# Gate tiles squared ahead inside the group loop, and weight parts in three pairs, in a two-layer FNet/attention kernel

## The chip, the cores and the metric

One core of a Trainium2 chip runs the whole program. The metric is the device time of one execution in microseconds; lower is better. Engines are called by the names that the profile uses: PE (TensorE: matmuls), ACT (ScalarE), DVE (VectorE), POOL (GpSimd) and SP (SyncE, which here only issues transfers). PEclk is the share of full clock granted to PE.

## The reference, cut to what matters

Two layers on 256 tokens of width 2048, with a second stream of 256 context tokens. The change lies in layer 0, the Fourier layer, in its gate and in its output projection, and in the rows of `silu(c) @ ada_w` that are needed later.

```python
def _fourier_branch(h, w_in, w_mix):            # w_in: 2048 x 8192
    u, z = jnp.split(h @ w_in, 2, axis=-1)      # z is the gate: 4096 columns
    ug = u.reshape(b, n, 16, 256)
    f = jnp.fft.fft2(ug, axes=(1, 3), norm='ortho').real
    f = jnp.einsum('bngc,gcd->bngd', f, w_mix).reshape(b, n, D_BRANCH)
    return f * jax.nn.silu(z)

for i in range(DEPTH):
    shift, scale, gate = jnp.split((jax.nn.silu(c) @ ada_w[i] + ada_b[i])[:, None, :], 3, axis=-1)
    h = _rmsnorm(x, norm_g[i]) * (1 + scale) + shift
    ...
    x = x + gate * (y @ w_out[i])
```

All weights are float32. The kernel keeps the precision by splitting each operand in a high and a low part and adding three products, `mm3`: high·high, high·low, low·high.

## The kernel before

**The loop over 16 groups.** After an opening stage, the loop over g computes one group of 256 branch columns per turn, some 14.4 us each (118 to 332 us of the span). Per turn SP loads two 1 MB tiles of the Fourier half of the input weights (`raw<-in_wu`), DVE folds them (`wm`, and in place `wp`, L134), ACT casts the high parts (`wmh`, `wph`, L66), DVE subtracts for the low parts (L67), and PE multiplies. Two more operands come by way of ACT and DVE: the mixing weights of the turn (`m` is loaded by ACT's queue, DVE adds and subtracts to `mt`, ACT casts it to a high part `mh<-mt`, L66, and PE transforms it with the constants `ch`, `cl`; the results are `pqh`, `sp`), and PE's sums (`mh<-ps` and `aph<-ps`, L66; `ml` and `apl` are DVE's low parts, L67). PE mixes both, and ACT copies `gsb` (L694) and a column of `ft` (L700) out. In turns 8 to 11 a 1 MB gate tile (`wz0`) is also loaded into the shared ring of three `raw` buffers, and ACT squares it (L161, 128x2048) with a sum per row, in place. The sum gives the power-of-two-like scale under which the 16-bit split of a gate tile is made (POOL adds over the partitions, L165 `tot`; DVE makes the scale `up` and its inverse `dn`, L170 and L171; ACT multiplies `dn` with a second factor, L173).

**Shared gate tiles.** Four `wz0` tiles (kg 0 to 3) give four gate blocks of 128 columns each (332 to 382 us). The 16 operands hs(k) come from transfers that POOL issues (`act<-in_xT`, L762): DVE scales (L768), ACT casts to 16 bits (L769), DVE subtracts (L770). Each tile is split in two halves by ACT (L179) and DVE (L180). The 1 MB loads alternate between the ring `raw` and a second ring `rawz` of three buffers.

**Units.** Then come 28 tiles `wz` (382 to 672 us) and 32 tiles `wo0` (672 to 1004 us), each with 48 matmuls of 128x512. The tile after next is loaded, squared by ACT into the buffer that will hold its own high part (L161 `w<-raw`), summed by POOL, and split by ACT and DVE (L179, L180). High and low parts take turns in the few `ws` buffers, so the square of a tile waits for the matmuls of an earlier unit. Between the splits DVE computes rows of `ada_w` (L730, a custom multiply and sum, 128x1024 each; `ada_step` issues up to two steps per unit), from tiles that come through the same two rings, and multiplies the outputs (L780, L870).

**What sets the order.** Each engine runs its instructions in one list, and a waiting instruction holds all behind it. The list is made by a scheduler from the program's order, with `issue_after(x)` as a bound: what stands inside is not listed ahead of x. SP's and POOL's transfers are issued in order too.

Of the kernel before, what the change touches and what calls it, by code (L numbers as in the profile page):

```python
# [10 lines left out]
F32 = mybir.dt.float32  # L11
# [21 lines left out]
def tile_dit(ctx: ExitStack, tc: tile.TileContext, a: dict, out: bass.AP):  # L33
# [134 lines left out]
    def scale(tot, down=None, tag="", bufs=6):  # L168
        u, d = small("up" + tag, bufs=bufs), small("dn" + tag, bufs=bufs)
        V.tensor_scalar(u.bitcast(I32), tot.bitcast(I32), -0.5, float(204 << 23), op0=ALU.mult, op1=ALU.add)  # L170
        V.reciprocal(d, u)  # L171
        if down is not None:
            S.activation(d, d, AF.Copy, scale=down)  # L173
        return u, d
# [397 lines left out]
    w4 = adap.tile([P, 4], F32, name="w4")  # L572
    hsc = adap.tile([P, 2, KT, 2], F32, name="hsc")
    hq = [small("hq") for _ in range(3)]
    squares(hsc[:, 0], gs0, hq[0], 64.0)
    squares(hsc[:, 1], sh0, hq[1], 1.5)
    V.tensor_tensor(hq[2], hq[0], hq[1], op=ALU.add)
    hup, hdn = scale(total(hq[2]), None, "h", 1)
    V.tensor_scalar(hsc[:, 0], gs0, hup, None, op0=ALU.mult)
    V.tensor_scalar(hsc[:, 1], sh0, hup, None, op0=ALU.mult)  # L580
# [11 lines left out]
    for g in range(G):  # L592
# [36 lines left out]
        if g == 13:  # L629
            w1 = small("w1", bufs=1)  # L630
            V.tensor_reduce(w1, w4, axis=AX.X, op=ALU.add)
# [8 lines left out]
        if g > 3:  # L640
            with after_evac(g - 1), tc.issue_after(m_end[0]), tc.issue_after(m_end[1]):
                w[1]["p"] = split_part("p", v)
        oa = {} if g > 2 else ou[g]
# [36 lines left out]
        evacs.append((last_cast[0], last_sub[0]))  # L680

# [34 lines left out]
    def ada_jobs():  # L716
        for pieces in ((0,), (1, 2, 3)):
            for kh in range(2):
                cb = adap.tile([P, 2, 1024], F32, tag="cb", name="cb")
                with tc.issue_after(hs_end[2]):  # L720
                    nc.gpsimd.dma_start(cb, a["crow"][:, kh].broadcast_to([P, 2, 1024]))
                with tc.issue_after(hs_end[1]):
                    S.activation(cb, cb, AF.Silu)  # L723
                for i in pieces:
                    for fg in range(8):
                        w = ada_raw(a["adw"][i, kh, fg])
                        for f in range(2):
                            wf = w[:, f * 1024 : f * 1024 + 1024]
                            for s in range(2 if i < 3 else 1):
                                V.tensor_tensor_reduce(junk, wf, cb[:, s], 1.0, 0.0, ALU.mult, ALU.add, acc[:, i, kh, fg * 2 + f, s : s + 1])  # L730
# [10 lines left out]
    junk = adat.tile([P, 1056], BF16, name="junk")[:, 0:1024]  # L741
    acc = adat.tile([P, 4, 2, KT, 2], F32, name="acc")
    YA = 8
    with tc.tile_pool(name="yp", reuse_waits="tile", bufs=33 - YA) as ypool, tc.tile_pool(name="zp", reuse_waits="tile", bufs=3) as zp:
        ys = [act() if b < YA else ypool.tile([P, 512], F32, tag="y", name="y") for b in range(NB)]
        hs = []
        hs_end = [None] * 3
        turn = [0]

        def raw6(src, view=lambda t, s: ((t, s),)):  # L750
            turn[0] += 1
            pool, nm = (rawp, "raw") if turn[0] % 2 else (zp, "rawz")
            t = pool.tile([P, D], F32, tag=nm, name=nm)
            for d, s in view(t, src):
                last_dma[0] = nc.sync.dma_start(d, s).ins
            return t

        ada_raw = raw6
# [14 lines left out]
        yq = adap.tile([P, NB], F32, name="yq")  # L773
# [26 lines left out]
        ready = {}  # L800

        def fetch(n):
            if n >= len(jobs):
                return
            nm, at_, i = jobs[n]
            if nm == "wz":
                t = raw6(a["wz"][at_])
            else:
                v = a["wo0"][at_[0] // 8, i * 8 : i * 8 + 8].rearrange("g p (j b f) -> p g j b f", j=2, b=8)[:, :, :, at_[0] % 8]
                t = raw6(v, lambda t, s: [(t.rearrange("p (g j f) -> p g j f", g=8, j=2)[:, :, j], s[:, :, j]) for j in range(2)])  # L810
            h, q = half16(), small("wq")
            squares(h, t, q)
            ready[n] = t, h, *scale(total(q), hdn if nm == "wz" else ydn[i])

        def weights(n):
            t, wh, up_, dn = ready.pop(n)
            wl = half16()
            split16(wh, wl, t, up_)
            fetch(n + 2)
            return wh, wl, dn  # L820

        o4 = [psum() for _ in range(4)]
        for kg in range(4):
            wr = raw6(a["wz0"][kg])
            wh, wl = half16(), half16()
            for i in range(2):
                make_hs(kg * 4 + i * 2)
                q = slice(i * 1024, (i + 1) * 1024)
                with tc.issue_after(hs_end[0]) if kg else nullcontext(), tc.issue_after(hs_end[1]) if kg else nullcontext():
                    split16(wh[:, q], wl[:, q], wr[:, q], u4)  # L830
                make_hs(kg * 4 + i * 2 + 1)
            for j in range(4):
                k = kg * 4 + j
                for b in range(4):
                    q = slice(j * 512 + b * P, j * 512 + (b + 1) * P)
                    mm3(o4[b], wh[:, q], wl[:, q], hs[k][0], hs[k][1], k == 0, k == KT - 1)
        for b in range(4):
            with tc.issue_after(last_dma[0]):
                nc.sync.dma_start(ys[b], fd[b])
        for b in range(4):  # L840
            z_out(b, o4[b], d4)
        fetch(0)
        fetch(1)
        for b in range(4, NB):
            wh, wl, dn = weights(b - 4)
            with tc.issue_after(last_dma[0]):
                nc.sync.dma_start(ys[b], fd[b])
# [9 lines left out]
            with tc.issue_after(hs_end[0]) if b < 8 else nullcontext():  # L857
                ada_step(1)
# [4 lines left out]
        def evac0(b, i, o, dn):  # L863
            t = xin[b]
            gd = adap.tile([P, 2], F32, tag="gd", name="gd", bufs=4)
            V.tensor_scalar(gd, gt0[:, b, :], dn, None, op0=ALU.mult)
# [22 lines left out]
        for n, (b, i) in enumerate(outs):  # L889
            if n == 0:  # L890
                y_scale(1)
            wh, wl, dn = weights(n + NB - 4)
# [10 lines left out]
            ada_step(0 if n > 29 else 2 if n > 19 else 1)  # L903
# [14 lines left out]

    def x1_turn(tb, c):
# [4 lines left out]
        S.copy(t, o)  # L924
        nc.sync.dma_start(x1d[tb, :, c * 512 : (c + 1) * 512], t)

    row_sums(3)
# [8 lines left out]
    with tc.issue_after(st_end[0]):  # L936
# [6 lines left out]
        for c, tb in ((0, 0), (0, 1), (1, 0), (1, 1), (2, 0)):  # L943
            x1_turn(tb, c)
# [593 lines left out]
```

## Time and profile before

| | us |
|---|---|
| median of three runs | 1788.28 |
| lowest and highest run | 1785.28, 1790.5 |
| the profiled execution, own time | 1785.5 |
| its span, first to last instruction | 1783.7 |
| PE busy in the span | 1731.1 (97%) |
| DVE, ACT, POOL busy | 1398.2, 1039.3, 256.6 |

| stage | from, to (us of the span) |
|---|---|
| opening | 0, 118 |
| group loop | 118, 332 |
| shared gate tiles | 332, 382 |
| 28 wz units | 382, 672 |
| 32 wo0 units | 672, 1004 |
| norm, and layer 1 | 1004, 1784 |

The profiled execution is 2.8 us below the median and close to the lowest run. A row of the table of windows gives, for a stretch of the span, the busy time and the number of instructions of each engine, the granted clock and the share of the DMA engines. In a timeline row the bracket is the idle time of that engine ahead of the instruction, and what ended it. In the list of waits a row gives the waiting instruction, whom it waited for, the sum, the count, and the longest.

### The profile page before, as it was taken

What the parts mean: (1) busy time and instruction counts of PE and PEld (TensorE: products, weight loads), DVE (VectorE), ACT (ScalarE), POOL (GpSimd) and SP (SyncE); (2) the same over time, 40 slices, a digit from 0 to 9 for tenths busy, and PEclk for the clock granted to TensorE, in tenths of its full rate; (3) what the DMA queues carried; (4) which work ended last, traced back from release to release, by engine and by line L of the source; (5) the groups of instructions that cost most, each with busy time, mean ns of one, the idle gap of its engine ahead of it and who ended that gap; (6) DMA issues with size and microseconds to landing.
All of it is one profiled execution on the core that took longest, in us unless ns stands there. A gap on an engine that the chain in (4) does not pass through costs nothing. (4 is left out here: it accounts for less than half of the span.)

```text
span 1783.7 us, 25965 instructions
## 1 busy us (share of the span) xinstructions
PE 1731.1 (97%) x9449; PEld 1204.6 (68%) x9449; DVE 1398.2 (78%) x2415; ACT 1039.3 (58%) x1708; POOL 256.6 (14%) x277
## 2 busy tenths in 40 slices
PE   6999999999999999999999999999999999999997
PEld 4679999644444444444444588788888888887886
DVE  5779778789889997953587463989999999997455
ACT  5544544485565656444334343777888888887343
POOL 0002111211000001100101000322212212234001
PEclk9999999999999999999999999999999999999999
DMA  9998898857777798654468323578898988888554
GB/s 393 417 340 230 234 279 237 288 214 283 275 261 264 259 327 256 204 164 130 131 226 275 112 97 104 174 179 219 213 208 211 216 208 208 210 216 262 197 179 142
DMA packets 267777, 403.06 MB, mean 226 GB/s; under 512 B 152641, under 2 KB 218577, under 8 KB 236161
## 3 DMA queue, kind: packets, MB, share of 16 engines
q1 hardware_dynamic: 243584, 363.39, 64.9%
q0 software_dynamic: 19920, 31.06, 6.9%
q10 hardware_dynamic: 4144, 6.95, 1.2%
q8 instruction: 74, 1.21, 0.3%
q14 instruction: 55, 0.44, 0.1%
HBM read 356.26 MB, written 12.59 MB: 207 GB/s over the span
## 5 line engine op out<-in xcount | busy, mean ns | idle before, releaser
L67 DVE TENSOR_TENSOR wl<-raw,wh 128x1024 fp32r<-128x1024 f32 x205 | 272.3, 1334 | 112.0 <-ACT wh L66 109.3
L66 ACT CAST wh<-raw 128x1024 fp32r<-128x1024 f32 x205 | 214.2, 1046 | 136.9 <-PE ps L80 123.6
L730 DVE CUSTOM_DVE_ANT_0 junk<-rawz,cb 128x1024 bf16<-128x1024 f32 x200 | 244.0, 1220 | 8.5 <-ACT cb L723 5.6
L80 PE MATMUL ps<-act,w 128*128 128x512 f16 x640 | 243.5, 381 | 0.5 <-DVE act L770 0.5
L79 PE MATMUL ps<-act,w 128*128 128x512 f16 x640 | 239.4, 381 | 4.0 <-ACT w L179 2.2
L81 PE MATMUL ps<-act,w 128*128 128x512 f16 x640 | 239.6, 379 | 0.2 <-DVE w L180 0.2
L1203 PE MATMUL ps<-h,wh 128*128 128x512 f32 x512 | 187.1, 403 | 0.0
L81 PEld LDWEIGHTS <-w 128*128 128x128 f16 x1024 | 100.2, 98 | 127.9 <-DVE w L180 6.8
L79 PEld LDWEIGHTS <-w 128*128 128x128 f16 x1024 | 100.4, 98 | 125.2 <-ACT w L179 3.3
L80 PEld LDWEIGHTS <-w 128*128 128x128 f16 x1024 | 100.4, 98 | 120.6 <-issue 0.8
L180 DVE SCALAR_TENSOR_TENSOR w<-raw,up,w 128x2048 f16<-128x2048 f32 (+1 forms) x58 | 131.8, 2274 | 51.5 <-PE ps L80 45.1
L161 ACT ACTIVATE w<-raw 128x2048 f16<-128x2048 f32 x54 | 102.8, 1904 | 94.2 <-PE ps L81 50.0
L81 PE MATMUL ps<-y,w 128*128 128x512 f16 x384 | 145.2, 379 | 4.0 <-DVE w L180 4.0
L80 PE MATMUL ps<-y,w 128*128 128x512 f16 x384 | 145.4, 379 | 0.0
L79 PE MATMUL ps<-y,w 128*128 128x512 f16 x384 | 144.9, 379 | 0.0
L1205 PE MATMUL ps<-h,wl 128*128 128x256 f32 x512 | 138.4, 281 | 0.0
L179 ACT ACTIVATE w<-raw,up 128x2048 f16<-128x2048 f32 (+1 forms) x58 | 112.1, 1935 | 23.3 <-DVE up L170 22.2
L80 PE MATMUL ps<-wl,h 128*128 128x512 f32 x320 | 125.1, 391 | 0.3 <-DVE wl L67 0.3
L81 PE MATMUL ps<-wh,h 128*128 128x512 f32 x320 | 123.8, 390 | 0.0
L79 PE MATMUL ps<-wh,h 128*128 128x512 f32 x320 | 122.4, 397 | 0.0
L165 POOL PARTITION_ALL_REDUCE tot<-wq x60 | 42.6, 713 | 541.5 <-ACT w L161 456.8
L1257 DVE SCALAR_TENSOR_TENSOR f<-p,sm,f 128x512 f16<-128x512 f32 x128 | 103.1, 824 | 12.0 <-ACT f L1256 11.8
(380 smaller groups left out, 4051.7 us busy)
## 6 DMA issues: line engine op xcount, KB each, us to landing
raw<-in_wz SPq DMA_DIRECT2D x65, 1024.0 KB, 5.3
rawz<-in_adw SPq DMA_DIRECT2D x56, 1024.0 KB, 5.1
raw<-in_awp SPq DMA_DIRECT2D x32, 1024.0 KB, 12.8
raw<-in_wq SPq DMA_DIRECT2D x32, 1024.0 KB, 5.2
raw<-in_wu SPq DMA_DIRECT2D x32, 1016.0 KB, 7.3
raw<-in_wo SPq DMA_DIRECT2D x54, 512.0 KB, 5.7
raw<-in_wo1b SPq DMA_DIRECT2D x16, 1024.0 KB, 4.9
act<-in_xT POOLq DMA_DIRECT2D x32, 256.0 KB, 6.3
```

The source lines that it names most:

```text
L66: last_cast[0] = S.copy(h, src).ins
L67: last_sub[0] = eng.tensor_tensor(l, src, h.bitcast(F32), op=ALU.subtract).ins
L79: PE.matmul(o, wh, xh, start=start, stop=False)
L80: PE.matmul(o, wh, xl, start=False, stop=False)
L81: return PE.matmul(o, wl, xh, start=False, stop=stop).ins
L161: sq_ins[0] = S.activation(dump, src, AF.Square, scale=scale, accum_out=col).ins
L179: last_cast[0] = S.activation(h, src, AF.Copy, scale=up).ins
L180: last_sub[0] = V.scalar_tensor_tensor(l, src, up, h, op0=ALU.mult, op1=ALU.subtract).ins
L730: V.tensor_tensor_reduce(junk, wf, cb[:, s], 1.0, 0.0, ALU.mult, ALU.add, acc[:, i, kh, fg * 2 + f, s : s + 1])
L1203: PE.matmul(o[0], wh[:, q], hx1[k], start=k == 0, stop=k == KT - 1)
L1205: PE.matmul(o[0][:, 0:N], wl[:, q], hx1[k][:, 0:N], start=False, stop=False)
L1257: V.scalar_tensor_tensor(f[:, 512:1024], pt[tb], sm[:, tb : tb + 1], f[:, 0:512], op0=ALU.mult, op1=ALU.subtract)
```

## The change

**Squares ahead.** Six gate tiles are squared inside the loop: the four `wz0` tiles and the first two `wz` tiles. Each is read in an even turn from 4 to 14 into a buffer of its own (`cb`), not into the ring, and squared in two halves in the odd turn after it. The tiles are loaded once more when they are split, so two tiles are read twice that were read once before. The sums of gs0 and sh0 and their scale move from ahead of the loop into turns 6 and 7.

**Rings.** Weight tiles now all come through `raw`, `ada_w` tiles all through `rawz`. The gate's blocks 0 to 10 (0 to 7 before) are loaded into `act` buffers, and these are taken one by one, not all ahead of the shared tiles.

**Three pairs.** High and low part are taken as a pair at the split, and squares are dumped into a buffer of their own (`sqd`). With the six `ws` buffers three pairs stand at once. Per unit ACT splits tile n and then squares tile n+1; tile n+3 is loaded. The multiply of `dn` (L173) moves from ACT to DVE.

**Other.** Two `ada_step`s are issued in units b = 7, 10, 13; in the 32 `wo0` units the second steps stand in other places, none in the first four. The gate row times the two `dn` of y is made once (`gty`). One transpose of `x1` moves ahead of the last row sums.

```diff
@@ scale
         if down is not None:
-            S.activation(d, d, AF.Copy, scale=down)
+            V.tensor_scalar(d, d, down, None, op0=ALU.mult)
@@ ahead of the loop
-    squares(hsc[:, 0], gs0, hq[0], 64.0)
-    squares(hsc[:, 1], sh0, hq[1], 1.5)
...
+    def read_ahead(j):
+        src = a["wz0"][j] if j < 4 else a["wz"][j - 4]
+        ahead[0] = adap.tile([P, D], F32, tag="cb", name="cb")
+        nc.sync.dma_start(ahead[0], src)
+
+    def square_ahead(j):
+        for i in range(2):
+            t = ahead[0][:, i * 1024 : (i + 1) * 1024]
+            squares(t, t, w6[:, j * 2 + i : j * 2 + i + 1])
@@ in the loop
-        if g == 13:
-            ...
-            u4, d4 = scale(total(w1), hdn, "4", 1)
-        if 8 <= g < 12:
-            t = raw(a["wz0"][g - 8])
-            squares(t, t, w4[:, g - 8 : g - 7])
...
         evacs.append((last_cast[0], last_sub[0]))
+        if g in (4, 6, 8, 10, 12, 14):
+            with tc.issue_after(last_dma[0]):
+                read_ahead(g // 2 - 2)
+        elif g > 4:
+            with after_evac(g):
+                square_ahead(g // 2 - 2)
...
@@ units
-            pool, nm = (rawp, "raw") if turn[0] % 2 else (zp, "rawz")
+        def ada_raw(src):
+            t = zp.tile([P, D], F32, tag="rawz", name="rawz")
...
-            h, q = half16(), small("wq")
-            squares(h, t, q)
-            ready[n] = t, h, *scale(total(q), hdn if nm == "wz" else ydn[i])
+        def measure(n):
+            if n < 2:
+                ready[n] = first[n]
+            elif n < len(jobs):
+                q = small("wq")
+                with tc.issue_after(last_cast[0]):
+                    squares(sqd, loaded[n], q)
+                    tot = total(q)
+                with tc.issue_after(last_sub[0]):
+                    ready[n] = scale(tot, hdn if jobs[n][0] == "wz" else None)
 
         def weights(n):
-            t, wh, up_, dn = ready.pop(n)
-            wl = half16()
-            split16(wh, wl, t, up_)
-            fetch(n + 2)
+            up_, dn = ready.pop(n)
+            wh, wl = half16(), half16()
+            split16(wh, wl, loaded.pop(n), up_)
+            measure(n + 1)
+            fetch(n + 3)
...
-                with tc.issue_after(hs_end[0]) if kg else nullcontext(), tc.issue_after(hs_end[1]) if kg else nullcontext():
+                with tc.issue_after(hs_end[0] if kg else wp_end[1]), tc.issue_after(hs_end[1] if kg else wp_end[0]):
                     split16(wh[:, q], wl[:, q], wr[:, q], u4)
...
-                ada_step(1)
+                ada_step(2 if b in (7, 10, 13) else 1)
...
-            ada_step(0 if n > 29 else 2 if n > 19 else 1)
+            ada_step(0 if n < 4 or n > 28 else 2 if 4 < n < 9 or n > 24 else 1)
```

The first place is ACT in the loop. Before, in the third of the four turns with a gate tile, its square stands ahead of the casts `wmh` and `mh<-mt` (L66; in the turn ahead of it, it stands between `wmh` and a copy of `ft`, with `mh<-mt` behind that):

```order
L66 CAST mh_1459<-ps 127x2x127
L694 COPY gsb<-ps 128x256 x2
L700 COPY ft<-ps 128x2 x2
L161 ACTIVATE raw,w_1403<-raw 128x2048
L66 CAST wmh<-wm 128x1016
L66 CAST mh<-mt 128x512
L436 DMA m<-in_wm 128x512
L66 CAST aph<-ps 127x260
```

Now, in turn 5 and in each odd turn after it, two half squares stand behind the cast of `aph`, ahead of that of `pqh` (`pqh` and `sp` are parts of the mixing weights):

```order
L66 CAST wmh<-wm 128x1016
L66 CAST mh<-mt 128x512
L436 DMA m<-in_wm 128x512
L728 COPY ft<-ps 128x2 x2
L66 CAST wph<-raw 128x1016
L66 CAST aph<-ps 127x260
L161 ACTIVATE cb,w_1403<-cb 128x1024 x2
L66 CAST pqh<-ps 128x512
```

The square has moved from a place ahead of `wmh` and `mh<-mt` to one behind them and behind `aph`. On SP, each read of a gate tile still stands between two `raw<-in_wu` loads, but it goes into a buffer that no such load uses.

The second place is ACT where the loop ends and the shared tiles begin. L769 (now L804) makes the 16-bit halves of hs(k), two per k. Before, the first half of k = 1, the third in the list, is the last one ahead of the `mh<-ps` of turn 15:

```order
L769 ACTIVATE act<-act,hsc 128x256 x2
L694 COPY gsb<-ps 128x256 x2
L700 COPY ft<-ps 128x2
L701 DMA fd_1447<-ft 128x512
L700 COPY ft<-ps 128x2
L701 DMA fd_1448<-ft 128x512
L769 ACTIVATE act<-act,hsc 128x256
L66 CAST mh_1459<-ps 127x2x127
```

Now the split of the first shared tile comes first, and five halves stand ahead of that `mh`:

```order
L179 ACTIVATE w_4153<-raw,up_3882 128x1024 x2
L804 ACTIVATE act<-act,hsc 128x256 x2
L722 COPY gsb<-ps 128x256 x2
L804 ACTIVATE act<-act,hsc 128x256 x2
L728 COPY ft<-ps 128x2
L729 DMA fd_1433<-ft 128x512
L728 COPY ft<-ps 128x2
L729 DMA fd_1434<-ft 128x512
L804 ACTIVATE act<-act,hsc 128x256
L66 CAST mh_1445<-ps 127x2x127
L804 ACTIVATE act<-act,hsc 128x256
L66 CAST aph<-ps 127x260
```

So `mh` has moved behind the whole of k = 1 and half of k = 2.

The third place is ACT at the end of the shared tiles. Before, the squares of the first two `wz` tiles and their splits stand among the last halves of hs:

```order
L179 ACTIVATE w_4428<-rawz,up_3534 128x1024
L161 ACTIVATE w_4540,wq<-raw 128x2048
L161 ACTIVATE w_4552,wq<-rawz 128x2048
L769 ACTIVATE act<-act,hsc 128x256 x2
L179 ACTIVATE w_4540<-raw,up 128x2048
L173 ACTIVATE dn<-dn,dnh 128x1
L179 ACTIVATE w_4552<-rawz,up 128x2048
L769 ACTIVATE act<-act,hsc 128x256 x2
```

Now no square stands there, and the order of the units follows, split, then the square of the next tile (L815 and the `act,yq` rows make the gate's output and its square sum):

```order
L804 ACTIVATE act<-act,hsc 128x256 x4
L179 ACTIVATE w_4429<-raw,up_3882 128x1024
L804 ACTIVATE act<-act,hsc 128x256 x2
L179 ACTIVATE w_4549<-raw,up_4133 128x2048
L751 ACTIVATE cb<-cb 128x2048
L815 ACTIVATE act<-ps,dn_3883 128x512
L179 ACTIVATE w_4619<-raw,up_4142 128x2048
L815 ACTIVATE act<-ps,dn_3883 128x512 x3
L161 ACTIVATE sqd,wq<-raw 128x2048
L161 ACTIVATE act,yq<-act 128x512 x4
L179 ACTIVATE w_4695<-raw,up 128x2048
L161 ACTIVATE sqd,wq<-raw 128x2048
```

The two whole squares have left the stretch in which PE waits for halves of hs, and the splits of the first two units have moved behind nearly all of these halves.

More of the change, by code (lines that the diff above doesn't have):

```diff
@@ L569, in tile_dit, with scale_ahead @@
         fill_pe(len(fill))
-    w4 = adap.tile([P, 4], F32, name="w4")
+    w6 = adap.tile([P, 12], F32, name="w6")
     hsc = adap.tile([P, 2, KT, 2], F32, name="hsc")
-    hq = [small("hq") for _ in range(3)]
-    squares(hsc[:, 0], gs0, hq[0], 64.0)
-    squares(hsc[:, 1], sh0, hq[1], 1.5)
[L577 to L580, printed above, removed]
+    ahead, early = [None], {}
+    def read_ahead(j):
[6 more added lines that the diff above has]
+            squares(t, t, w6[:, j * 2 + i : j * 2 + i + 1])
+    def scale_ahead(j, n, tag):
+        w1 = small("w1", bufs=3)
+        V.tensor_reduce(w1, w6[:, j * 2 : (j + n) * 2], axis=AX.X, op=ALU.add)
+        return total(w1), tag
     fd = [dram.tile([P, 512], F32, name=f"fd{b}") for b in range(NB)]
@@ L771, in make_hs @@
             hs.append((hl[:, 0:512], hl[:, 512:1024]))
-        yq = adap.tile([P, NB], F32, name="yq")
+        yq = adat.tile([P, NB], F32, name="yq")
+        gty = [adat.tile([P, KT, 2], F32, name=f"gty{i}") for i in range(2)]
         yup, ydn, yy = [None] * 2, [None] * 2, []
@@ L891, in tile_dit @@
                 y_scale(1)
+                for d, y in zip(gty, ydn):
+                    V.tensor_scalar(d, gt0, y, None, op0=ALU.mult)
             wh, wl, dn = weights(n + NB - 4)
@@ L923, in x1_turn @@
         t = act()
-        S.copy(t, o)
+        turn_end[0] = S.copy(t, o).ins
         nc.sync.dma_start(x1d[tb, :, c * 512 : (c + 1) * 512], t)
-    row_sums(3)
+    with tc.issue_after(e), tc.issue_after(sq_end[0]):
+        x1_turn(0, 0)
+    with tc.issue_after(turn_end[0]):
+        row_sums(3)
     ssum = [const.tile([P, 4], F32, name=f"ssum{i}") for i in range(2)]
```

87 lines of the change are left out of this document (54 added, 33 removed).

## The prediction

> **What bounds the kernel now.** I read the page first, then PE's waits, then the stretches around them.
>
> ```profile
> span 1783.7 us, 25965 instructions
> PE 1731.1 (97%) x9449; PEld 1204.6 (68%) x9449; DVE 1398.2 (78%) x2415; ACT 1039.3 (58%) x1708; POOL 256.6 (14%) x277
> ```
>
> PE is busy 97% of the span, and the change leaves its matmuls as they are. So only two things can go: moments in which PE waits, and the slow clock behind some of them. PE's list of waits from 215 to 1020 us, the part that the change touches from its first gate tile to its last unit, has these rows:
>
> ```profile
> PE ps L79 <- ACT mh L66: 7.0, 3, 3.7
> PE ps L81 <- DVE w L180: 4.2, 4, 1.5
> PE ps L79 <- ACT w L179: 2.2, 1, 2.2
> PE ps L79 <- ACT act L769: 1.6, 1, 1.6
> PE ps L79 <- ACT ft L700: 1.2, 1, 1.2
> PE ps L885 <- ACT act L872: 1.0, 1, 1.0
> PE ps L80 <- DVE act L770: 0.5, 1, 0.5
> PE ps L80 <- DVE ml L67: 0.4, 1, 0.4
> ```
>
> They sum to 18.1 us. The clock adds to it; the table of windows shows it in PEclk, the third number from the end:
>
> ```profile
> 241.00:245.00 4.00, 4.00 (x23) 4.00 (x22) 2.01 (x3) 0.00 (x0) 0.00 (x0) 0.57 1.17 298
> 272.00:276.00 4.00, 3.44 (x29) 3.45 (x30) 3.98 (x7) 2.34 (x5) 1.46 (x3) 1.00 0.81 132
> 344.00:348.00 4.00, 1.83 (x7) 0.54 (x5) 1.16 (x1) 1.15 (x1) 0.00 (x0) 0.85 0.53 200
> 348.00:352.00 4.00, 4.00 (x15) 1.57 (x14) 3.47 (x9) 2.50 (x5) 0.00 (x0) 0.72 0.80 285
> ```
>
> Behind the wait of 3.7 us the clock is 0.57 for 4 us: 4 × 0.43 = 1.7 us lost. Behind that of 2.2 us at 346.86 it is 0.85 and then 0.72: 0.6 + 1.1 = 1.7 us. Behind that of 2.1 us at 272.56 it is 1.00. So about 21.5 us can go at most, 1.2% of the time.
>
> The Trainium skill, "TensorE: Matmul & The Clock Gate", Part 1, says that the clock halves after an idle window of about 3.4 us. The first and third place agree; at 346.86 a wait of 2.2 us was enough here, so the rule would value that wait at 1.7 us less. The rows decide.
>
> **The loop.** Here is ACT around the wait of 3.73 us, and PE's row:
>
> ```profile
> 236.25 1.91 ACT L161 ACTIVATE raw<-raw 128x2048 f32<-128x2048 f32 x1 [0.68 <-DMA raw<-in_wz]
> 238.15 1.02 ACT L66 CAST wmh<-wm 128x1016 fp32r<-128x1016 f32 x1
> 239.08 0.61 ACT L66 CAST mh<-mt 128x512 fp32r<-128x512 f32 x1
> ...
> 239.75 0.39 PE L79 MATMUL ps<-mh,ch 128*128 128x256 f32 x1 [3.73 <-ACT mh L66]
> ```
>
> ACT waited for the gate tile's transfer, squared for 1.9 us, and only then cast the two operands that PE wanted. The gate tiles cost in a second way: they hold one of three `raw` buffers. The wait at 272.56 comes from this: no square stands right ahead of it on ACT, but the `wu` tile that DVE folds there had to wait for the buffer of the last gate tile, and DVE for the `wu` tile:
>
> ```profile
> 265.32 1.22 DVE L134 TENSOR_TENSOR wm<-raw 128x1016 f32<-128x1016 f32 x1 [1.18 <-DMA raw<-in_wu]
> ```
>
> The next rows are the transfers ahead of the first gate tiles (118 to 200 us) and among them (200 to 262); the last number is the median time to landing:
>
> ```profile
> raw<-in_wu SPq DMA_DIRECT2D x9, 1016.0 KB, 6.2
> ...
> raw<-in_wu SPq DMA_DIRECT2D x8, 1016.0 KB, 8.1
> raw<-in_wz SPq DMA_DIRECT2D x3, 1024.0 KB, 4.9
> ```
>
> The change takes both reasons away: the buffer is the gate tile's own, and the squares stand behind `aph`. What goes is 1.2 + 3.7 + 2.1 + 0.4 = 7.4 us and 1.7 us of clock: **9.1 us**. What comes is six squares of some 2.3 us (1.91 by the row at 236.25 and the 0.24 to the next row twice, as an estimate), 14 us of ACT, and six reads. In the new place ACT has room, as the rows of one turn show:
>
> ```profile
> 225.07 0.59 ACT L66 CAST pqh<-ps 128x512 fp32r<-128x512 f32 x1 [2.48 <-PE ps L81]
> ...
> 228.91 1.05 ACT L66 CAST wph<-raw 128x1016 fp32r<-128x1016 f32 x1 [2.88 <-DMA raw<-in_wu]
> ```
>
> ACT stands still for 2.48 us ahead of `pqh`, so a square of 2.3 us nearly fits without a trace; if that cover were gone, `pqh` would be late by up to 2.3 us in each of six turns, ahead of a second idle of 2.88 us. For a read the bounds are nothing (it lands in the gaps of the transfers) and 4.9 us (its whole landing time falls on the next `wu` tile). I take nothing, since four such reads stood there before at a slot that held up more. So the loop gives 9.1, between 4 and 9.8 us.
>
> **The shared tiles.** First what goes. The split at 345.66 waited for a tile in the second ring:
>
> ```profile
> 331.52 0.51 ACT L769 ACTIVATE act<-act,hsc 128x256 f16<-128x256 f32 x1 [4.81 <-DVE act L768]
> 331.94 0.35 ACT L66 CAST mh<-ps 127x254 fp32r<-127x254 f32 x1
> ...
> 345.66 1.15 ACT L179 ACTIVATE w<-rawz,up 128x1024 f16<-128x1024 f32 x1 [4.08 <-DMA rawz<-in_wz]
> ...
> 368.90 1.90 ACT L161 ACTIVATE w<-raw 128x2048 f16<-128x2048 f32 x1
> ...
> 372.69 0.89 ACT L769 ACTIVATE act<-act,hsc 128x256 f16<-128x256 f32 x2
> ```
>
> Now that tile comes through `raw` with its neighbours, ahead of the `ada_w` loads, so 2.2 us and 1.7 us of clock go. The two squares from 368.90 to 372.69 leave, and with them the 1.6 and 0.5 us for halves of hs. Together **6.0 us**.
>
> Then what comes. The `mh` of turn 15 now has all of k = 1 and a half of k = 2 ahead of it. In the row at 331.52 the first half of k = 1 is itself waiting, through DVE, for its transfer, and PE already waits 1.1 us (the third of the `mh` waits). DVE's rows give both transfers:
>
> ```profile
> 331.01 0.88 DVE L768 SCALAR_TENSOR_TENSOR act<-act,hsc,r_bc 128x256 f32<-128x256 f32 x2 [4.60 <-DMA act<-in_xT]
> ...
> 333.75 0.88 DVE L768 SCALAR_TENSOR_TENSOR act<-act,hsc,r_bc 128x256 f32<-128x256 f32 x2
> ```
>
> Two more halves on ACT are 2 × 0.51 = 1.0 us; DVE's work for k = 2 starts 2.7 us after that for k = 1. So the new wait lies between nothing and 2.7 + 0.9 = 3.6 us more, with another 1.7 us if the clock falls. Against it, POOL issues these transfers behind matmuls that now stand some 19 places earlier in PE's order, about 2.4 us (45.11 us for 360 matmuls, in the row of 200 to 250 us under the rivals). I take 1.5 us. The splits of the first two units stand behind more halves than before: between nothing and the 2.0 us of one split; I take 1.0. So this stage gives 6.0 − 1.5 − 1.0 = **3.5 us**, between −1 and 6.5.
>
> **The units.** A unit lasts 290 / 28 = 10.36 us on PE, which never stops from 382 to 672:
>
> ```profile
> 382.00:672.00 290.00, 290.00 (x1345) 131.41 (x1344) 271.28 (x428) 170.76 (x225) 24.67 (x34) 1.00 0.78 280
> L180 DVE SCALAR_TENSOR_TENSOR w<-raw,up,w 128x2048 f16<-128x2048 f32 (+1 forms) x58 | 131.8, 2274 | 51.5 <-PE ps L80 45.1
> L161 ACT ACTIVATE w<-raw 128x2048 f16<-128x2048 f32 x54 | 102.8, 1904 | 94.2 <-PE ps L81 50.0
> ```
>
> Split and square both wait for PE to free a buffer, so a split can be ready at most 10.36 − 2.34 = 8.0 us ahead. This lead is used up twice: from 718 to 737 by `ada` rows, and from 890 to 985, where DVE waits at the scale:
>
> ```profile
> L730 DVE CUSTOM_DVE_ANT_0 junk<-rawz,cb 128x1024 bf16<-128x1024 f32 x10 | 12.2, 1220 | 0.1
> ...
> L730 DVE DVE_READ_ACCUMULATOR2_ANT acc<- 128x1 f32 x10 | 0.8, 82 | 0.0
> ...
> 973.33 0.15 DVE L170 TENSOR_SCALAR up<-tot 128x1 int32<-128x1 int32 x1 [2.18 <-POOL tot L165]
> ...
> DVE up L170 <- POOL tot L165: 7.9, 5, 2.5
> DVE gd L866 <- ACT dn L173: 4.6, 2, 2.5
> ```
>
> (The first two rows are DVE by groups from 718 to 735, the third is one of its waits, the others are their sums from 890 to 985.) That gives the four waits `<- DVE w L180`, **4.2 us**. With three pairs the lead can grow to 8.0 + 10.36 = 18.4 us, more than what was missing; and the wait for ACT's `dn` is replaced by a DVE instruction of some 0.15 us, the size of the row at 973.33. The cost is on DVE: 0.15 us more per unit is 4.2 us in the wz stage, against 290 − 271 = 18.7 us that it is idle there. Its worst new place is 16 `ada` rows between the splits of tiles 28 and 29: 16 × (1.22 + 0.08) + 2.34 = 23 us, against 10.36 + 18.4 = 28.8 if the lead is full. I take no cost; the bounds are 5 us lost (lead at 8 us there) and none. So 4.2, between −1 and 5.
>
> The transpose ahead of the last row sums fills the wait of 1.0 us at L885, but the sums end the chain there: nothing.
>
> **Sum.** 9.1 + 3.5 + 4.2 = 16.8 us. The profiled execution took 1785.5 us and would take 1768.7; the median, 2.8 us above it, comes to **1771.5**.
>
> **Rivals.** (1) *The shared tiles eat their gain.* `mh` is late by 3.6 us more and the clock falls (1.7), and the transfers for k = 4 and on, now behind the last `tot` on POOL, hold PE for another us: 6.3 in place of 2.5, so 3.8 less, 1775.3; with a repeat of the stall at kg1, 1779. For it: the row at 331.52. Against it: transfers issued earlier.
>
> (2) *The lead does not grow.* DVE is busy 271 of 290 us, so it may never get two units ahead, and the waits for `w L180` stay: 4.2 less, 1775.7; with 5 us at the 16 rows, 1780. Against it: before, DVE held its 8.0 us and waited for PE, 45.1 us in all.
>
> (3) *The loop gains half.* A read delays a `wu` tile by 1 us in each of six turns: 6 less, 1777.5.
>
> (4) *Slower: the reads crowd out the loop's loads.* The DMA engines are busy here, as the last but one number shows:
>
> ```profile
> 200.00:250.00 50.00, 45.11 (x360) 44.69 (x359) 35.42 (x51) 26.10 (x47) 7.25 (x9) 0.97 0.86 255
> ```
>
> If each of six reads put its 4.9 us on the next `wu` tile, PE would wait 29.4 us: 12.6 more than the 16.8 gained, **1801**. It decides from 16.8 / 6 = 2.8 us per read. Against it: PE's old waits end at ACT, and of four reads only the held buffer and the square came through. The Trainium skill, "DMA: Bandwidth & Descriptors", section "Issuing engines are not separate DMA queues", says that transfers of all engines end up on the same 16 and interleave; by that a buffer of its own takes the wait for the slot away, not the bandwidth. The 8.1 us against 6.2 agrees, without telling the two apart.
>
> **Chances.** Forecast 0.55; (1) 0.15; (2) 0.10; (3) 0.11; (4) 0.07; something unseen of no effect 0.02. Runs of this kernel tell apart about 0.3%, 5.4 us: 1782.9 to 1793.6 is "same". (1), (2) and (3) reach it in part when two of them meet: same 0.11, slower 0.07, faster 0.82. The range goes from 1762 (the upper bounds, 9.8 + 6.5 + 5 = 21.3 us, give 1767, and the three runs lie 5 us apart) to 1782, where (1) to (3) end.
>
> **What would show it.** PE's waits for `mh` and `ft` at 221, 240 and 272 are gone, with clock 1.00 there, and `wu` lands in 6 to 7 us. At the end of the loop PE waits for `mh` or for the first halves of hs, 1 to 4 us, and none for a tile in `rawz`. From 382 to 1004 no wait `<- DVE w`, and the split's own wait falls. Wrong would be: new waits in turns 5 to 15 for `wm` or `pqh` (rivals 3 and 4), a clock below 1.00 near 332 (1), or waits for `w L180` near the 16 rows (2).

## The result and the profile after

| | before | after |
|---|---|---|
| median of five runs, us | 1786.99 | 1764.65 |
| lowest and highest | 1783.78, 1790.5 | 1759.88, 1766.58 |
| span of the profiled execution | 1783.7 | 1763.6 |

The ratio is 0.9871, with a 95% interval of 0.985 to 0.9892: 22 us faster by the medians, 20.1 by the two spans. The forecast was 1771.5, in a range of 1762 to 1782. The change did more than was expected of it. Of all the runs below one was slow, a run of `dn_act` at 2192.86 us with a granted clock of 0.754, and no median here counts it.

PE's list of waits from 215 to 1020 us held 18.1 us in eight rows before. Of the changed kernel these four rows are all:

```profile
PE ps L81 <- DVE w L180: 1.8, 1, 1.8
PE ps L928 <- ACT act L915: 0.6, 1, 0.6
PE ps L79 <- ACT w L179: 0.5, 1, 0.5
PE ps L998 <- DVE r4h L96: 0.4, 1, 0.4
```

The windows by stage (length, busy time of PE, PEld, DVE, ACT, POOL, clock, DMA share, GB/s) show PE without a gap through the loop, at the end of the loop, and at the first units, at full clock:

```profile
200.00:300.00 100.00, 100.00 (x831) 100.00 (x831) 86.73 (x128) 56.95 (x106) 19.12 (x22) 1.00 0.98 274
322.00:326.00 4.00, 4.00 (x24) 2.35 (x22) 3.30 (x14) 3.44 (x9) 2.26 (x5) 1.00 0.27 81
326.00:330.00 4.00, 4.00 (x22) 2.22 (x21) 3.76 (x10) 2.46 (x7) 4.00 (x9) 1.00 0.82 245
364.00:368.00 4.00, 4.00 (x21) 1.77 (x19) 4.00 (x7) 4.00 (x5) 0.00 (x0) 1.00 1.03 401
655.00:992.00 337.00, 334.76 (x1563) 153.11 (x1562) 232.94 (x406) 141.97 (x130) 33.23 (x48) 1.00 0.61 192
```

Where the time went is read from three of PE's matmuls that do the same work in both kernels: the mixing weights of turn 15, the first behind the 192 matmuls of the shared tiles (where the `wz` units begin), the last of the last `wo0` unit. Before, and then after:

```profile
316.01 0.28 PE L79 MATMUL ps<-mh,ch 128*128 128x256 f32 x1
...
382.36 0.38 PE L80 MATMUL ps<-act,w 128*128 128x512 f16 x1
...
1011.40 0.38 PE L81 MATMUL ps<-y,w 128*128 128x512 f16 x1
```

```profile
306.98 0.28 PE L79 MATMUL ps<-mh,ch 128*128 128x256 f32 x1
...
364.97 0.38 PE L79 MATMUL ps<-act,w 128*128 128x512 f16 x1
...
991.57 0.38 PE L81 MATMUL ps<-y,w 128*128 128x512 f16 x1
```

| | forecast | measured, profile against profile |
|---|---|---|
| loop | 9.1 | 316.01 − 306.98 = 9.0 |
| shared tiles | 3.5 | (382.36 − 364.97) − 9.0 = 17.4 − 9.0 = 8.4 |
| units | 4.2 | (1011.40 − 991.57) − 17.4 = 19.8 − 17.4 = 2.4 |
| behind them | 0 | 20.1 − 19.8 = 0.3 |

The transfers answer too. From 200 to 262 us, where the median landing of a `wu` tile was 8.1 us before, the changed kernel has:

```profile
raw<-in_wu SPq DMA_DIRECT2D x8, 1016.0 KB, 6.1
raw<-in_wu POOLq DMA_DIRECT2D x5, 508.0 KB, 6.9
cb<-in_wz SPq DMA_DIRECT2D x2, 1024.0 KB, 6.6
```

More is moved per us (a DMA share of 0.98 from 200 to 300 us, 0.86 from 200 to 250 before), and the `wu` tiles land sooner.

### The profile page after: what moved, and what is told of

Read it like the earlier page. It is cut to its first block, busy times and chain, and to the rows that moved or that the text cites. A ratio compares the mean times of both kernels' runs of the same rounds, so it can differ in the third digit from the quotient of the medians.

```text
span 1763.6 us, 25874 instructions
## 1 busy us (share of the span) xinstructions
PE 1725.5 (98%) x9449; PEld 1202.4 (68%) x9449; DVE 1404.5 (80%) x2448; ACT 1024.9 (58%) x1659; POOL 268.1 (15%) x277
## 5 line engine op out<-in xcount | busy, mean ns | idle before, releaser
L66 ACT CAST wh<-raw 128x1024 fp32r<-128x1024 f32 x205 | 214.2, 1046 | 136.0 <-PE ps L80 126.8
L758 DVE CUSTOM_DVE_ANT_0 junk<-rawz,cb 128x1024 bf16<-128x1024 f32 x224 | 273.4, 1221 | 14.6 <-DMA rawz<-in_adw 8.5
L80 PE MATMUL ps<-act,w 128*128 128x512 f16 x688 | 260.8, 379 | 0.0
L81 PE MATMUL ps<-act,w 128*128 128x512 f16 x688 | 258.2, 379 | 1.8 <-DVE w L180 1.8
L79 PE MATMUL ps<-act,w 128*128 128x512 f16 x688 | 258.0, 379 | 0.5 <-ACT w L179 0.5
L179 ACT ACTIVATE w<-raw,up 128x2048 f16<-128x2048 f32 (+1 forms) x68 | 129.0, 1899 | 215.5 <-PE ps L80 191.5
L180 DVE SCALAR_TENSOR_TENSOR w<-raw,up,w 128x2048 f16<-128x2048 f32 (+1 forms) x68 | 151.1, 2223 | 29.6 <-ACT w L179 29.5
L165 POOL PARTITION_ALL_REDUCE tot<-wq x58 | 53.0, 914 | 488.7 <-ACT sqd L161 488.7
L80 PE MATMUL ps<-y,w 128*128 128x512 f16 x336 | 127.2, 379 | 0.0
L81 PE MATMUL ps<-y,w 128*128 128x512 f16 x336 | 127.2, 379 | 0.0
L79 PE MATMUL ps<-y,w 128*128 128x512 f16 x336 | 127.0, 379 | 0.0
L1253 PEld LDWEIGHTS ps<-h,wh 128*128 128x128 f32 x512 | 96.3, 188 | 20.6
```

The lines of the kernel that those rows point to most:

```text
L66: last_cast[0] = S.copy(h, src).ins
L79: PE.matmul(o, wh, xh, start=start, stop=False)
L80: PE.matmul(o, wh, xl, start=False, stop=False)
L81: return PE.matmul(o, wl, xh, start=False, stop=stop).ins
L165: GP.partition_all_reduce(tot, col, P, bass_isa.ReduceOp.add)
L179: last_cast[0] = S.activation(h, src, AF.Copy, scale=up).ins
```

## The experiments

Nine of the twelve kernels are the new one with a part or two taken back; `before_buf` is the old one with one part of the new, and `b31` and `y_first` look for more. Times are medians; ratios are against the kernel before, run on the same chip.

**The loop: order on ACT, or the slot in the ring?** The forecast took both reasons together. Three runs part them. `early` squares each tile whole at the old place, ahead of `mh<-mt`, out of the tile's own buffer:

```diff
+        if g > 4 and g % 2:
+            j = g // 2 - 2
+            V.memset(w6[:, j * 2 + 1 : j * 2 + 2], 0.0)
+            squares(ahead[0], ahead[0], w6[:, j * 2 : j * 2 + 1])
         if g > 4:
             with tc.issue_after(m_end[2]):
                 w.append({"m": split_part("m", f3[1][1])})
...
-        elif g > 4:
-            with after_evac(g):
-                square_ahead(g // 2 - 2)
```

> The changed kernel, with each gate tile squared whole again at the old place in the odd turn, ahead of mh<-mt, but out of the tile's own buffer. Theory A (what stood ahead of mh on ACT made most of the loop's 9.1 us): in the turns 5, 7, ... 15 PE waits for mh by 1 to 4 us each, 6 to 15 us in all, with a clock below 1.00 behind the longest. Theory B (the held ring slot made it): under 2 us of waits in all, the time within 3 us of the changed kernel's 1764.65.

1769.07 us, ratio 0.9887 (0.9867 to 0.9907). From 118 to 322 us PE waits for nothing at all, and the first `wz` unit starts at 365.1, as in the changed kernel (365.0). Theory A falls: no wait came. The median lies 4.4 us above the changed kernel's, where theory B allowed 3, but the kernel before was 2.9 us slower on this chip too (1789.89 against 1786.99), and the intervals of the two ratios overlap. `ring` does the opposite: squares behind `aph`, tiles in the shared ring.

```diff
     def read_ahead(j):
-        ahead[0] = adap.tile([P, D], F32, tag="cb", name="cb")
-        nc.sync.dma_start(ahead[0], src)
+        ahead[0] = raw(src)
...
+        if g > 4 and g % 2:
+            read_ahead(g // 2 - 2)
```

> The changed kernel, with each gate tile read into the shared ring of three raw buffers again, in the odd turn, and squared at the new place behind aph. Theory A (ACT's order): under 2 us of waits in the loop. Theory B (the slot): wu tiles land in 8 us or more in place of 6.3, and PE waits 5 us or more in all in the turns after a read.

1804.94 us, ratio 1.0087 (1.0064 to 1.0109): slower than before the change. PE's waits from 118 to 345 us:

```profile
PE ps L79 <- ACT mh L66: 20.4, 8, 4.9
```

The whole loop's end has moved back by 29 us (the first shared matmul at 351.6 in place of 322.3), the clock's loss included. The landing time was not what told it: 6.4 us from 200 to 262 us, since a load that waits for a slot is not yet issued. DVE's wait for it does:

```profile
240.49 1.22 DVE L134 TENSOR_TENSOR wm<-raw 128x1016 f32<-128x1016 f32 x1 [1.35 <-DMA raw<-in_wu]
```

One thing was not clean: with the tile read later, the scheduler put the squares of two turns ahead of `mh<-mt` too. The waits right behind those two make 8.2 us; the other six, 12.2 us in all, have no square of a gate tile just ahead of the cast. And six tiles stood in the ring, not four, each held until behind `aph`, so 29 us is no measure of the old loss. `before_buf` is the clean run: the old kernel, with nothing else changed than the buffer and the bound on its load.

```diff
         if 8 <= g < 12:
-            t = raw(a["wz0"][g - 8])
+            t = adap.tile([P, D], F32, tag="cb", name="cb")
+            with tc.issue_after(last_dma[0]):
+                nc.sync.dma_start(t, a["wz0"][g - 8])
             squares(t, t, w4[:, g - 8 : g - 7])
```

> The kernel before, with the four gate tiles of turns 8 to 11 read into a buffer of their own; squares whole, at the old place ahead of mh<-mt, everything else as before. Theory B (the held ring slot made the loop's waits): PE's waits for mh and ft from 215 to 300 us, 7 us before, fall under 1 us, the last mixing of the loop starts 8 to 9 us earlier. Theory A (the squares ahead of mh made them): at least 4 us of the waits stay.

1777.36 us, ratio 0.9945 (0.9922 to 0.9969). In its profile PE is never idle from 215 to 300 us, with three of the four squares still ahead of `mh<-mt` in ACT's list, and of its waits for `mh` up to 325 us, that of turn 15 among them, 0.2 us is left:

```profile
215.00:300.00 85.00, 85.00 (x708) 85.00 (x707) 72.98 (x106) 47.12 (x83) 14.70 (x19) 1.00 0.94 257
```

```profile
PE ps L79 <- ACT mh L66: 0.2, 1, 0.2
```

The last mixing starts at 306.7 us, 9.3 earlier than before. A buffer of its own, at the same place in the program and with the same bytes moved, was worth the loop's 9 us. That is shown.

**The shared tiles.** `rawz` puts kg 1 and kg 3 back into the second ring:

```diff
-            wr = raw(a["wz0"][kg])
+            wr = ada_raw(a["wz0"][kg]) if kg % 2 else raw(a["wz0"][kg])
```

> The changed kernel, with the shared tiles kg 1 and kg 3 loaded into the second ring rawz again. Theory A (that ring takes memory which the loop holds to its end, so its loads start late): the split of kg 1 waits for its transfer, PE waits about 2 us, and 1.7 us of clock go, 3 to 5 us in all. Rival (the wait came from the slow loop ahead of it): under 0.5 us.

1772.09 us, ratio 0.9901 (0.9878 to 0.9924). ACT and PE, with the clock behind the wait:

```profile
337.27 2.19 ACT L179 ACTIVATE w<-rawz,up 128x1024 f16<-128x1024 f32 x2 [4.53 <-DMA rawz<-in_wz]
```

```profile
PE ps L79 <- ACT w L179: 5.2, 2, 4.5
```

```profile
338.00:342.00 4.00, 3.52 (x9) 1.33 (x10) 3.37 (x5) 2.09 (x4) 0.00 (x0) 0.50 1.04 413
342.00:346.00 4.00, 4.00 (x16) 1.61 (x15) 3.27 (x7) 2.22 (x4) 0.00 (x0) 0.78 1.01 422
```

4.5 us of waiting and 2.0 + 0.9 = 2.9 us of clock; the first unit starts 7.2 us late. Theory A stands, and even more is lost than before (2.2 + 1.7), because PE now arrives earlier: the first `rawz` load is issued at 327.12 here and at 327.16 in the changed kernel, while there the four tiles come through `raw`, issued from 298 to 314. `late_sq` squares only the four `wz0` tiles ahead (reads in turns 4 to 10) and the first two `wz` tiles among the halves of hs:

```diff
-        if g in (4, 6, 8, 10, 12, 14):
+        if g in (4, 6, 8, 10):
...
+            if n < 2:
+                q = small("wq")
+                squares(sqd, loaded[n], q)
+                ready[n] = scale(total(q), hdn)
```

> The changed kernel, with only the four wz0 tiles squared ahead; the first two wz tiles are squared among the halves of hs again. Theory A: PE waits 1.5 to 3 us for halves of hs or for the splits between 322 and 370 us. Rival: the squares alone cost nothing there, because the tiles are loaded earlier now than before: under 0.5 us.

1776.9 us, ratio 0.9934 (0.9909 to 0.996). Two waits of PE make 6.2 us, twice what theory A allowed. ACT's rows show that the 1.9 us of the square is the smaller part:

```profile
343.40 1.91 ACT L161 ACTIVATE sqd<-raw 128x2048 f16<-128x2048 f32 x1 [6.83 <-DMA raw<-in_wz]
345.22 0.19 ACT L161 ACTIVATION_READ_ACCUMULATOR sqd<-raw 128x1 f32 x1
345.31 0.89 ACT L804 ACTIVATE act<-act,hsc 128x256 f16<-128x256 f32 x2
346.11 1.13 ACT L179 ACTIVATE w<-raw,up 128x1024 f16<-128x1024 f32 x1
...
359.03 1.91 ACT L161 ACTIVATE sqd<-raw 128x2048 f16<-128x2048 f32 x1 [3.58 <-DMA raw<-in_wz]
```

The square waits for its tile at the head of ACT's queue, and hs and the split behind it wait with it. `kg0` takes back the bound that puts the first shared split behind the casts of `wph`:

```diff
-                with tc.issue_after(hs_end[0] if kg else wp_end[1]), tc.issue_after(hs_end[1] if kg else wp_end[0]):
+                with tc.issue_after(hs_end[0]) if kg else nullcontext(), tc.issue_after(hs_end[1]) if kg else nullcontext():
```

> The changed kernel, with the split of the first shared tile no longer bound behind the casts of wph. Theory A (the bound moves PE's matmuls so that POOL can issue the transfers of hs(1) and hs(2) earlier, which is why mh was not late): hs(1) lands later against the last mixing of the loop, and PE waits 1 to 5 us for mh or ml near 316 to 325 us. Rival (the transfers land early because the weight loads are out of their way): under 0.5 us.

1766.8 us, ratio 0.9881 (0.9858 to 0.9903). No wait of PE over 0.1 us from 316 to 325: the bound is not what spared the `mh` of turn 15. In the changed kernel ACT's rows are

```profile
318.27 0.51 ACT L804 ACTIVATE act<-act,hsc 128x256 f16<-128x256 f32 x1 [1.18 <-DVE act L803]
321.27 0.37 ACT L66 CAST mh<-ps 127x254 fp32r<-127x254 f32 x1 [2.49 <-PE ps L81]
```

and all that the forecast feared ahead of `mh` is done 2.5 us before PE's sum is there. The transfer for k = 1 landed 3.2 us after its issue, where it took 8.4 us before; three loads of shared tiles had been issued from 320 to 324 us then, two of them ahead of it. That these loads slowed it is argued from the rows, and no run shows it alone: now, too, one such load was on its way and two more were issued within 3.2 us. Nor is the short landing sure. In ten of the eleven profiles of the changed kernel and its variants (`ring` apart) it took 3.0 to 3.8 us; in that of `old_rows` it took 7.7 us, and there `mh` is late just as the forecast feared. DVE and then ACT wait for hs, and PE waits 1.6 us at 323.0:

```profile
318.25 0.88 DVE L803 SCALAR_TENSOR_TENSOR act<-act,hsc,r_bc 128x256 f32<-128x256 f32 x2 [4.36 <-DMA act<-in_xT]
```

```profile
322.22 0.51 ACT L804 ACTIVATE act<-act,hsc 128x256 f16<-128x256 f32 x1 [0.96 <-DVE act L803]
322.63 0.35 ACT L66 CAST mh<-ps 127x254 fp32r<-127x254 f32 x1
```

`old_rows` differs from the changed kernel only behind this place, so the landing seems to vary between executions; what delays it stays open.

**The units.** Four parts of the change could have ended the waits for `w L180`: the lead, the places of the `ada` steps, the rings, the multiply of `dn`. `one_lead` takes the first back, `old_rows` the second, `old_units` both, `dn_act` the fourth.

```diff
                 q = small("wq")
+                held[n] = half16()
                 with tc.issue_after(last_cast[0]):
-                    squares(sqd, loaded[n], q)
+                    squares(held[n], loaded[n], q)
...
-            wh, wl = half16(), half16()
+            wh = held.pop(n) if n in held else half16()
+            wl = half16()
```

> The changed kernel, with the square of a tile dumped into the buffer of its own high part again (taken at the square), as before. Theory A (the lead of two units is what ends the waits of the units): the splits end at most 8 us ahead, and PE waits for w L180 sum to 4 us or more between 365 and 992 us, 6 or more where 16 rows stand between two splits. Rival (the new places of the ada rows end them): PE's waits there stay at 2 to 3 us.

1771.92 us, ratio 0.9911 (0.9887 to 0.9935). The lead fell less than meant, from 16.4 us at most to 13.5, not to 8: the old order of split, square and load was not restored with the buffer. PE's waits from 365 to 990 us stay near 668 us, but there they grow from 2.2 to 4.4 us:

```profile
PE ps L81 <- DVE w L180: 2.8, 1, 2.8
PE ps L79 <- ACT w L179: 1.7, 1, 1.7
```

From the first matmul of the `wo0` units to their last it takes 340.4 us, 336.5 in the changed kernel and 339.0 before. So theory A holds at one place and not at several: the lead is worth something where it is used up, and the four old waits do not come back with a shorter one.

```diff
-                ada_step(2 if b in (7, 10, 13) else 1)
+                ada_step(1)
...
-            ada_step(0 if n < 4 or n > 28 else 2 if 4 < n < 9 or n > 24 else 1)
+            ada_step(0 if n > 29 else 2 if n > 19 else 1)
```

> The changed kernel, with the ada steps in the units in which they stood before. If the lead alone ends the waits: no wait of PE for w over 1 us except at the y scale near 668 us, as in the changed kernel. If the new places are needed too: waits of 1 us and more return in the second half of the wo0 units, 3 us or more in all.

1764.8 us, ratio 0.987 (0.985 to 0.9891): no loss, and one wait of 0.7 us in these stages. The wait of 1.6 us for `mh` at 323.0 us, ahead of them, is the one shown above. `old_units` has both edits.

> The changed kernel, with both the lead of one unit and the old places of the ada steps, each of which alone left no wait but those near 668 us. Theory A (each of the two covers the same waits): together undone, waits for w of 1 us and more return at several units, 4 to 9 us in all. Rival (a third part of the change, the rings or the multiply of dn on DVE, ended them): nothing but the wait near 668 us.

1764.61 us, ratio 0.9882 (0.9858 to 0.9906). One wait, again near 668 us:

```profile
PE ps L81 <- DVE w L180: 2.2, 1, 2.2
```

So neither the new places nor the full 16.4 us of lead are needed to end the four old waits. `dn_act` has one line:

```diff
-            V.tensor_scalar(d, d, down, None, op0=ALU.mult)
+            S.activation(d, d, AF.Copy, scale=down)
```

> The changed kernel, with the multiply of dn back on ACT. If the move to DVE matters: DVE waits for ACT ahead of the products with gd, a few us in all, and PE waits for w somewhere from 365 to 992 us, over 1 us more than now. Rival (nothing waits for dn there, since the dn of wo0 needs no second factor now): PE's waits stay at 2 to 3 us, the time within 3 us of the changed kernel.

1767.09 us, ratio 0.9889 (0.9859 to 0.9919); PE's waits are those of the changed kernel without its row of 0.5 us. The rival holds, in the presence of the other parts. Of the four parts the rings are left (that tile n+3 is loaded in place of n+2, and that a square stands behind the split, was not taken back either), and there the old trace has a row that the forecast did not read. ACT's waits from 700 to 990 us, before:

```profile
ACT w L161 <- PE ps L81: 55.2, 12, 5.2
ACT w L161 <- DMA raw<-in_wo: 40.5, 7, 9.7
...
ACT w L161 <- DMA rawz<-in_wo: 15.4, 3, 8.3
```

and in `old_units`, in the same stretch, no wait for a transfer is among the rows:

```profile
ACT w L161 <- PE ps L80: 95.7, 22, 6.5
ACT w L179 <- DVE up L170: 32.5, 23, 3.4
```

Before, weight tiles and `ada` tiles took turns in both rings. SP's own waits from 890 to 985 us, where three of the four old waits of PE lie, show what held its list of loads (L755 is the load into either ring, `acc` the sum that an `ada` tile is read for):

```profile
SPq L755 <- DVE acc L730: 21.5, 6, 5.3
SPq L755 <- DVE w L180: 19.6, 6, 5.7
```

A `wo0` tile's load stood in that list behind loads that waited until DVE's `ada` rows had freed a slot, so its square came late, then `tot`, then the split: a fault of the kind seen in the loop. In `old_units`, from 865 to 970 us, the waits for `acc` are 2.6 us. No run mixes the rings in the new kernel, so for the units this stays argued.

**What is left near 668 us.** `b31` was to take the `ada` rows out of the way of the split of tile 29:

```diff
-                ada_step(2 if b in (7, 10, 13) else 1)
+                ada_step(2 if b in (7, 10, 13) else b < 31)
...
-            ada_step(0 if n < 4 or n > 28 else 2 if 4 < n < 9 or n > 24 else 1)
+            ada_step(0 if n < 4 or n > 28 else 2 if 3 < n < 9 or n > 24 else 1)
```

> The changed kernel, with no ada step in the last wz unit (b = 31) and a second one in wo0 unit 4 in its place. Theory A (the split of tile 29 waits for the scale of y, and that for the last product y, which stands behind ada rows on DVE): the one long wait of PE at 668 us, 2.2 us, is gone or under 0.5 us. Rival (16 rows by themselves fill DVE): the wait falls by less than 1 us.

1766.34 us, ratio 0.9878 (0.986 to 0.9896), and 1.8 us of wait stay: a miss that says nothing of the theory, because the scheduler listed as many rows between the splits of tiles 28 and 29 as before. `y_first` binds them:

```diff
-                ada_step(2 if b in (7, 10, 13) else 1)
+                ada_step(2 if b in (7, 10, 13) else b < 30)
...
-            ada_step(0 if n < 4 or n > 28 else 2 if 4 < n < 9 or n > 24 else 1)
+            with tc.issue_after(last_sub[0]):
+                ada_step(0 if n < 4 or n > 28 else 2 if n < 10 or n > 24 else 1)
```

> The changed kernel, with no ada step in the last two wz units, two in each of the wo0 units 4 to 9, and every step of the wo0 units bound behind the split of its unit, so that no ada row stands on DVE between the last y product and the split of tile 29. In the run b31 the rows had only changed their place in the program, not in DVE's list: the last y product was still at 658.88, 3.9 us after its input. Theory A (the chain over the last y product is what the split of tile 29 waits for): the wait of 1.8 us of PE is gone or under 0.5 us, the stage of the wo0 units is 2 us shorter. Rival (the chain is too long even without rows): over 1 us stays.

From 365 to 990 us PE waits for nothing, and from the first `wo0` unit to its last matmul it takes 333.9 us in place of 336.5. Theory A stands. The median is 1762.73, ratio 0.9869 (0.9849 to 0.989): by time it cannot be told from the changed kernel's 0.9871.

## Why the prediction was right, point by point

**The bound** was right: PE's waits and the clock behind them. The list fell from 18.1 to 3.3 us, of which 2.2 are new, near 668 us, and in this profile no slow clock is left from 118 to 1020 us. The two spans differ by 20.1 us, within the 21.5; the medians differ by 22.3, a little over it, since the bound was read from one execution.

**The loop**: the size was right (9.1, measured 9.0), the mechanism half wrong. The step "ACT waited for the gate tile's transfer, squared for 1.9 us, and only then cast the two operands" named what PE's row named. `early` and `before_buf` show that a square ahead of `mh<-mt` costs nothing when its tile is there in time and the next `wu` tile has its slot. The slot in the ring was the whole. Whether it acted at 221 and 240 through the next `wu` tile, which the forecast saw at 272.56, or through the gate tile, for whose late transfer ACT waited 0.68 us with the casts behind it, no run parts. One term stood in the wrong stage: the 0.4 us for `ml` is a wait at 316.89, behind the loop's last mixing weights. The price of a square was right: two halves and their sums take 2.2 us (ACT, 322.21 to 324.40), although the 0.24 us that the estimate added is not in the rows shown for it. The six reads cost nothing, so rivals (3) and (4) fell; but `ring` shows how near the slower side was: the same reads, in the ring, made the kernel 0.9% slower than before.

**The shared tiles** were mis-sized: 3.5 forecast, 8.4 measured. The waits that were to go went (4.3 us), as `rawz` and `late_sq` show for their causes. What came, 1.5 for `mh` and 1.0 for the first two units, measured nothing in this profile, and the old waits of 1.1 us for `mh` and 0.4 for `ml` went too. The clock was worth more than 1.7: for 328 matmuls PE is busy 60.4 us from 316.01 to 382.36 before, and 57.9 us from 306.98 to 364.97 now, 2.5 less. The term for `mh` took the old landing time of the transfer, 8.4 us, where 3.2 came; that it measured nothing is partly luck, since `old_rows` shows a wait of 1.6 us there. Of the POOL queue (rival 1) nothing came: the transfer of k = 4 was issued behind the `tot` at 323.5, and no wait followed. The first unit's split was 0.95 us ahead.

**The units** were mis-sized the other way: 4.2 forecast, 2.4 measured. The four old waits went, as forecast, if not for the reason given. The step that failed is "16 × (1.22 + 0.08) + 2.34 = 23 us, against 28.8 if the lead is full". The lead was nearly as full as it gets (15.8 us at tile 28; 16.4 at most, where the forecast had 18.4), and still the split of tile 29 came 2.3 us late. DVE's rows show why:

```profile
650.59 1.23 DVE L758 CUSTOM_DVE_ANT_0 junk<-rawz,cb 128x1024 bf16<-128x1024 f32 x1 [2.91 <-DMA rawz<-in_adw]
...
658.65 1.22 DVE L758 CUSTOM_DVE_ANT_0 junk<-rawz,cb 128x1024 bf16<-128x1024 f32 x1
659.80 0.69 DVE L816 TENSOR_TENSOR y<-y,act 128x512 f32<-128x512 f32 x1
...
663.17 0.15 DVE L170 TENSOR_SCALAR upy<-tot 128x1 int32<-128x1 int32 x1 [0.27 <-POOL tot L165]
...
666.01 2.35 DVE L180 SCALAR_TENSOR_TENSOR w<-raw,up,w 128x2048 f16<-128x2048 f32 x1
```

Between the two splits the scale of the second half of y (`upy`) stands in DVE's list, and it needs the last gate block, which PE finished at 655. No lead reaches across that point; the rows then pushed the product to 659.8, and the split behind it. The sum counted DVE's work, and not what else had to happen first. The lead at unit 13, behind the first `upy`, fell to 2.3 us in the same way.

**The rest**: the transpose at L885 was put at nothing, and 1.0 us of wait became 0.6 and a new 0.4; right.

**The sum** came near in part by luck: the shared tiles gave 4.9 us more and the units 1.8 less than forecast, for reasons that the forecast did not have, and these misses cancel in part.

**The clock** was priced by the rows and not by the rule of the Trainium skill ("TensorE: Matmul & The Clock Gate", Part 1), and rightly so far as a wait shorter than the rule's window can cost clock: in `late_sq` one of 2.5 us did. But 1.7 us is no fixed price for a wait of 2.2 us, as the last section shows.

```profile
362.00:366.00 4.00, 3.08 (x8) 1.15 (x9) 3.61 (x10) 1.77 (x3) 1.24 (x3) 0.60 0.68 209
```

## What to carry to other kernels

Where two kinds of load share a ring, ask for each foreign tile how long it holds its slot, from issue to last reader, and which load stands behind it: its price is not the engine time of its reader, but the lateness of the next load, and the row that shows it is a wait for a transfer that was issued late, not one that flew long. The engine named by the consumer's wait (here ACT) need not be the cause; a run that changes the buffer alone, or the order alone, settles it with few lines. And before an order is made to run further ahead, look for the points that no lead can cross, such as a scale over all of the previous stage, and keep the engine's queue free just behind them.

## What the runs showed of the hardware that was not expected

The DMA engines ran the loop at a share of 0.98 (274 GB/s from 200 to 300 us) with no wait of PE, where 0.86 (255 GB/s) with waits had looked like a limit: bytes were not what the loop was short of (`before_buf` moved the same bytes as before, at 0.94, without the waits). And the clock fell to 0.50 for 4 us behind a wait of 4.5 us (`rawz`), to 0.60 behind one of 2.5 us (`late_sq`), but stayed at 1.00 behind one of 2.1 us in the loop before.

The length alone does not tell it. PE has the same wait near 668 us, 1.8 us for the same split, in the changed kernel and in `kg0`, which differs only ahead of it. Behind it the clock was 1.00 in the one and 0.62 in the other, and 17 matmuls started in 4 us, or 11:

```profile
668.00:672.00 4.00, 3.58 (x17) 1.68 (x18) 3.39 (x8) 3.65 (x3) 0.56 (x1) 1.00 1.00 395
```

```profile
669.00:673.00 4.00, 3.70 (x11) 1.39 (x12) 3.39 (x8) 3.66 (x3) 0.49 (x1) 0.62 0.99 391
```

In layer 1, at a place that the change does not touch, waits of 2.2 us left the clock at 1.00 in the changed kernel (1139.0 us) and took it to 0.57 for 4 us in `y_first` (1136.6 us). So a wait of about 2 us costs its length and, in some executions and not in others, some 1.7 us of clock (4 × 0.43). What decides it, no run here shows.
